# A hybrid attention layer: a differential head's output transposes moved two fillings later, the latent heads' squares summed by ScalarE, latent keys scaled as they leave PSUM

## The chip, the cores and the metric

The kernel runs on one core of one Trainium2 chip. The metric is device time in microseconds of one execution: the median of a few runs, with one more run that was profiled. The traces below are of that profiled run.

## The reference, cut to what matters

One encoder layer over 512 positions of width 2048. Its attention has two groups of 8 heads that share one input projection and one output projection; a SwiGLU feed-forward network follows. All arithmetic is float32.

```python
h = rms_norm(x, g_norm1) * (1 + sc1) + sh1
proj = h @ w_in
...
# differential heads: two softmaxes, one subtracted from the other
a = p[:, 0] - lam * p[:, 1]
a_out = rms_norm(a @ v, g_subln) * (1 - lambda_init)
# latent heads: query and key come from low-rank latents, both are normed
q_m = rms_norm((rms_norm(cq, g_q_a) @ w_q_b), g_q_mla)      # 192 = 128 + 64 rotary
kv = rms_norm(ckv, g_kv_a) @ w_kv_b                         # per head 128 key, 128 value
k_m = rms_norm(concat([k_nope, k_pe]), g_k_mla)             # mean of squares over 192
b_out = latent_attention(q_m, k_m, v_m)
mix = concat([a_out, b_out]) @ w_out
```

The norm of a latent key needs the sum of squares of its 128 own columns plus that of the 64 shared rotary columns, then a power of -0.5, and multiplies the key with it.

## The kernel before, in words

Float32 products are made of three matmuls on parts: a high part `hi` (ScalarE, L89) and a remainder `lo` (VectorE or GpSimd, L97) of each weight chunk, against the same two parts of the activations (`mm3`, L241 to L243).

The order of TensorE's instructions is the order in which the program writes them (`ORDERED` holds TensorE alone). On the other engines the framework's scheduler chooses an order, by program order among the instructions whose inputs and buffers it takes to be ready; so an instruction can stand in a queue ahead of one that the program writes earlier.

The attention part weaves two streams on TensorE. One is the heads' own work, written as a string of steps (`DIFF_STEPS` for a differential head, `MLA_STEPS` for a latent one): `s0` to `s3` are the scores of four blocks of queries, `t` the transposes of the probabilities, `v` the product with the values, `n` the norm of the next head's queries and keys, `o` the next head's operands, `e` the finish of the head before. The other stream is the filling, `F`: projections (`projections`), of which each `F` runs as many matmuls as its share of `DIFF_FILL` or `MLA_FILL` allows. Nine `F` share 26 us in a differential head.

`values` ends a block with a chain: ScalarE squares z with a sum over its columns (L738), GpSimd scales, adds and takes the power (L739 to L741) and multiplies z (L742). `finish` (step `e`) transposes the four z of a head on TensorE (L748, `ps_zT`) and splits the result (L610, L611).

`diff_norm` puts 8 multiplications (L666) and the power of the sums (L260, L261) of a coming head on GpSimd.

`mla_project(pr)` is run by the filling once for each of four pairs of latent heads. It projects queries (`qb`, 4 PSUM banks of tag `acc`), copies them out (`qm`), makes the rotary tails on GpSimd (L765 to L768, L827; eight `dup` buffers, which the pair before gives back when its second head's tails are transposed, L623), squares them (L831), reduces the squares on VectorE (L832), and takes the power on GpSimd (L834 to L836). Then it projects keys and values (`kvb`, the same 4 banks), and for each of four blocks squares the key (L844), reduces (L845), copies the value out (L847) and copies the key out (L813 through `copy`, `kn`). GpSimd adds the rotary squares (L853), takes the power (L260, L261), and multiplies `kn` (L857) and the rotary key (`kpt`, L859). Both PSUM tags, `acc` and `tmp`, have 4 banks. After the second and the fourth pair (pr 1 and 3) the filling goes straight on with a part of the output projection (`out_half`, `ps_o`), which takes 4 banks of `acc` again; after the first and the third it waits for the heads.

Of the kernel before, what the change touches and what calls it, by code (L numbers as in the profile page):

```python
# [12 lines left out]
AF = mybir.ActivationFunctionType  # L13
ALU = mybir.AluOpType
AX = mybir.AxisListType
# [3 lines left out]
P = 128  # L19
# [179 lines left out]
def hybrid_layer(ctx, tc, a, out):  # L199
    nc = tc.nc  # L200
    act, dve, pool, pe, sp = nc.scalar, nc.vector, nc.gpsimd, nc.tensor, nc.sync
# [23 lines left out]
    def bank(tag, name):  # L225
        return psum.tile([P, 512], F32, tag=tag, name=name)
# [31 lines left out]
    def rsqrt(dst, src, scale, eps=EPS):  # L258
        n = src.shape[-1]
        pool.tensor_scalar(out=dst, in0=src, scalar1=scale, scalar2=eps, op0=ALU.mult, op1=ALU.add)  # L260
        pool.tensor_tensor(out=dst, in0=dst, in1=mhalf[:, :n], op=ALU.pow)  # L261
# [145 lines left out]
    i = 0  # L407
    for kind in LOADS:
# [4 lines left out]
        else:  # L413
            t, b = divmod(i, 4)
# [35 lines left out]
    for t in range(NT):  # L450
        for b in range(4):
            sq = st[1].tile([P, 512], F32, tag="sq", bufs=2, name="sq1")
# [10 lines left out]
    def raw_tile(name="raw_in"):  # L463
        return sh[1].tile([P, 384], F32, tag="rin", bufs=16, name=name)

    def project(pss, lhs, width, chunks, k0=0, n=None, first=True, last=True, fine=False):

        n = len(lhs) if n is None else n
        kc = k0
        for key in chunks:  # L470
            wh, wl = W.get(key)
            nk = wh.shape[1]

            def mm(t, i):
                hh, hl = lhs[kc + i]
                mm3(pss[t][:, :width], hh[:, tsl(t)], hl[:, tsl(t)], wh[:, i], wl[:, i],
                    first and kc + i == k0, last and kc + i == k0 + n - 1)

            if kc + nk < k0 + n:
                for i in range(nk):  # L480
                    for t in range(NT):
                        mm(t, i)
                        if fine:
                            yield 3 * width * 0.000424
                    if not fine:
                        yield 12 * width * 0.000424
            else:
                for t in range(NT):
                    for i in range(nk):
                        mm(t, i)  # L490
                    if t % 2 or fine:
                        yield (1 if fine else 2) * 3 * nk * width * 0.000424
            kc += nk
# [96 lines left out]
    def sm(n, tag, bufs=4):  # L590
        return const.tile([P, n], F32, tag=tag, bufs=bufs, name=tag)
# [4 lines left out]
    def dup_tile(name):  # L596
        return sh[1].tile([P, 2, 2, 64], F32, tag="dup", bufs=8, name=name)
# [161 lines left out]
    def rope(dst, src, tb, t, nh):  # L759

        tmp = sh[1].tile([P, 2, 2, 32], F32, tag="rt", bufs=1, name="rt")
        s4 = src.rearrange("p h (s n) -> p h s n", s=2)
        o4 = dst.rearrange("p h (s n) -> p h s n", s=2)
        for i in range(2):
            pool.tensor_tensor(out=tmp[:, :nh, i, :], in0=s4[:, :, 1 - i, :],  # L765
                               in1=tb[1][:, t, i, :].unsqueeze(1).broadcast_to([P, nh, 32]), op=ALU.mult)
        pool.tensor_tensor(out=o4, in0=s4, in1=tb[0][:, t].unsqueeze(1).broadcast_to([P, nh, 2, 32]), op=ALU.mult)
        pool.tensor_tensor(out=o4, in0=o4, in1=tmp[:, :nh], op=ALU.add)  # L768
# [40 lines left out]
    def copy(by_act, dst, src):  # L809
        if by_act:  # L810
            act.copy(out=dst, in_=src)
        else:
            dve.tensor_copy(out=dst, in_=src)  # L813

    def mla_project(pr):
        pss = [bank("acc", "ps_in") for _ in range(NT)]
        yield from project(pss, latT["cq"], 384, [("qb", pr, 0), ("qb", pr, 1)], fine=True)
        qn, qp = [], []
        rs = sm(2 * NT, "rsq", 3)
        for t in range(NT):  # L820
            q = raw_tile("qm")
            copy(Q_ACT[t], q, pss[t][:, :384])
            q = q.rearrange("p (h n) -> p h n", h=2)
            qn.append(q)
            d = dup_tile("qpe")
            rope(d[:, :, 0, :], q[:, :, NOPE:], qtab, t, 2)
            pool.tensor_copy(out=d[:, :, 1, :], in_=d[:, :, 0, :])  # L827
            qp.append(d)
        for t in range(NT):
            sq = wk[1].tile([P, 384], F32, tag="sq", bufs=2, name="sqm").rearrange("p (a b) -> p a b", a=2)  # L830
            act.activation(sq, qn[t], AF.Square)  # L831
            dve.tensor_reduce(out=rs[:, 2 * t:2 * t + 2], in_=sq, axis=AX.X, op=ALU.add)  # L832
        rs2 = rs.rearrange("p (t h) -> p t h", t=NT)
        pool.tensor_scalar(out=rs, in0=rs, scalar1=1.0 / QKH, scalar2=None, op0=ALU.mult)  # L834
        pool.tensor_tensor(out=rs2, in0=rs2, in1=epsq.unsqueeze(2).broadcast_to([P, NT, 2]), op=ALU.add)
        pool.tensor_tensor(out=rs, in0=rs, in1=mhalf[:, :2 * NT], op=ALU.pow)  # L836
        pss = [bank("acc", "ps_in") for _ in range(NT)]
        yield from project(pss, latT["ckv"], 512, [("kvb", pr)], fine=True)
        kn, kp, v = [], [], []
        rk = sm(2 * NT, "rsk", 2)  # L840
        for t in range(NT):
            pv = pss[t].rearrange("p (h s n) -> p h s n", h=2, s=2)
            sq = wk[1].tile([P, 384], F32, tag="sq", bufs=2, name="sqm")[:, :256].rearrange("p (a b) -> p a b", a=2)
            act.activation(sq, pv[:, :, 0, :], AF.Square)  # L844
            dve.tensor_reduce(out=rk[:, 2 * t:2 * t + 2], in_=sq, axis=AX.X, op=ALU.add)  # L845
            vr = sh[1].tile([P, 2, P], F32, tag="v", bufs=8, name="vr")
            act.copy(out=vr, in_=pv[:, :, 1, :])  # L847
            v.append(vr)
            k = raw_tile("kn")[:, :256].rearrange("p (h n) -> p h n", h=2)
            copy(K_ACT[t], k, pv[:, :, 0, :])  # L850
            kn.append(k)
        rk2 = rk.rearrange("p (t h) -> p t h", t=NT)
        pool.tensor_tensor(out=rk2, in0=rk2, in1=sskpe.unsqueeze(2).broadcast_to([P, NT, 2]), op=ALU.add)  # L853
        rsqrt(rk, rk, 1.0 / QKH)
        for t in range(NT):
            r = rk[:, 2 * t:2 * t + 2].unsqueeze(2)
            pool.tensor_tensor(out=kn[t], in0=kn[t], in1=r.broadcast_to([P, 2, P]), op=ALU.mult)  # L857
            d = dup_tile("kpt")
            pool.tensor_tensor(out=d, in0=kpe[:, t:t + 1, :].unsqueeze(1).broadcast_to([P, 2, 2, 64]),  # L859
                               in1=r.unsqueeze(3).broadcast_to([P, 2, 2, 64]), op=ALU.mult)  # L860
            kp.append(d)
        pairs[pr] = (qn, qp, kn, kp, v, rs)
# [123 lines left out]
    def between(us, n):  # L986
        fill.run(us)
        for _ in range(n):
            next(side, None)
# [9 lines left out]
    for h in range(H):  # L999
        cur = diffs[h]  # L1000
        for step in DIFF_STEPS.split():
            kind, i = step[0], int(step[1:] or 0)
            if kind == "F":
                between(DIFF_FILL[h] / DIFF_STEPS.count("F"), DIFF_SIDE[h])
            elif kind == "n":
# [17 lines left out]
    for g in range(H + 1):  # L1023
# [4 lines left out]
        for step in MLA_STEPS.split():  # L1028
            kind, i = step[0], int(step[1:] or 0)
# [35 lines left out]
    def tmp(name):  # L1065
        return fo[1].tile([P, S], F32, tag="tmp", bufs=4, name=name)
# [25 lines left out]
    for b in range(4):  # L1092
        tag = next_tag()
        spare[0] = "tmp" if tag == "acc" else "acc"
        if b == 0:
            assert tag == "acc"
            pss = half[0]
        else:
            pss = [bank(tag, "ps_o") for _ in range(NT)]
        j0 = 0 if b == 1 else 4  # L1100
        for i, _ in enumerate(project(pss, mixT, 512, [("out", b, j) for j in range(j0, 8)], 2 * j0, KC - 2 * j0,
# [6 lines left out]
            if b == 1 and i % 2 and i < 16:  # L1108
                b2, t = 2 + i // 8, i % 8 // 2
# [8 lines left out]
        for t in range(NT):  # L1118
            residual(pss, b, t, gt1, pool if t in OUT_POOL and b < 3 else dve)
            sq = tmp("sq")  # L1120
# [19 lines left out]
    s3 = sx[1].tile([P, 8, 256], F32, name="s3")  # L1140
# [215 lines left out]
    for u in range(N_UNITS):  # L1356
# [4 lines left out]
        else:  # L1361
# [4 lines left out]
                         in_=ao.rearrange("p (f c) s -> p f (c s)", f=2))  # L1366
# [29 lines left out]
    for i, n in enumerate(PARTS):  # L1396
        for b in range(4):
            tag = next_tag()
            spare[0] = "tmp" if tag == "acc" else "acc"
            pss = [bank(tag, "ps_d") for _ in range(NT)]  # L1400
# [11 lines left out]
            for t in range(NT):  # L1412
                s = sums[t][b]
# [22 lines left out]
OUT_POOL = ()  # L1436
OUT_SPLIT = "alt"
Q_ACT = (0, 0, 1, 1)
K_ACT = (0, 0, 0, 0)
GATE_EARLY = True  # L1440
START_FILL = 5.2
DIFF_STEPS = "s0 F e s1 n F t0 F s2 v0 F t1 F s3 v1 F t2 F o0 v2 t3 F o1 v3 F"
DIFF_FILL = (26.0, 26.0, 26.0, 26.0, 26.0, 26.0, 26.0, 26.3)
DIFF_SIDE = (1, 2, 1, 2, 1, 2, 1, 1)
MLA_SIDE = (1, 2)
# [42 lines left out]
```

## Time and profile before

| | |
|---|---|
| median of 3 runs | 2294.44 us (2291.91 to 2295.82) |
| profiled execution, its own time | 2292.43 us |
| its span | 2290.6 us |
| TensorE matmul busy | 2183.1 us (95%) |
| VectorE, ScalarE, GpSimd busy | 71%, 41%, 18% |
| mean granted TensorE clock | 0.988 |

The span is the time between the first and the last instruction of the profiled run; 1.8 us of its time lie around it. TensorE sets the time where its row is full; where its row has gaps, the wait that ends each gap names the engine that was late. The differential heads run from about 240 to 560 us of the span, the latent heads from there to about 775 us. The feed-forward network fills the rest, from about 900 us on.

### The profile page before, as it was taken

The numbers are of one execution on the slowest core, as the hardware profiler recorded it, in microseconds if no ns is written. First come the engines' busy times: TensorE is split into PE (matmuls) and PEld (weight loads), VectorE is DVE, ScalarE is ACT, GpSimd is POOL, SyncE is SP. The second block draws the span as 40 slices with busy tenths as digits, with TensorE's granted clock in tenths as the row PEclk, the third lists the DMA queues.
The fourth block names the chain that finished last, engine by engine and source line by source line (L and its number), as shares of the span: only waits on it lengthen the run. The fifth ranks groups of instructions, "written<-read, shape, count | busy, mean of one in ns | idle before, by whom it ended". The sixth has DMA issues, their size and how long they took to land.

```text
span 2290.6 us, 35353 instructions
## 1 busy us (share of the span) xinstructions
PE 2183.1 (95%) x13878; PEld 1999.4 (87%) x13878; DVE 1625.7 (71%) x2290; ACT 945.3 (41%) x1569; POOL 418.2 (18%) x478
## 2 busy tenths in 40 slices
PE   2899999998989998999999999999999999999999
PEld 2799989997777776889999999999999877888887
DVE  5987788868998477857777777777777577232543
ACT  4423545556555323434444444444444522222221
POOL 0002533436444431000000000000000122222221
PEclk9899999999999998999999999999999999999999
DMA  9975345432433577233333333333333686242542
GB/s 295 330 224 152 92 146 157 136 90 84 161 121 119 173 251 256 85 128 120 130 120 123 110 127 117 119 116 129 120 127 123 218 274 215 101 133 98 165 138 101
DMA packets 270826, 344.99 MB, mean 151 GB/s; under 512 B 15006, under 2 KB 171143, under 8 KB 270531
## 3 DMA queue, kind: packets, MB, share of 16 engines
q1 hardware_dynamic: 267864, 338.18, 45.0%
q10 hardware_dynamic: 2794, 4.55, 0.6%
q8 instruction: 108, 1.77, 0.3%
q14 instruction: 60, 0.48, 0.1%
HBM read 322.71 MB, written 19.96 MB: 150 GB/s over the span
## 4 chain that ended last, share of the span: by engine, by line
PE 60%; DVE 8%; DMA 5%; issue 2%; ACT 1%; SPq 0%; POOL 0%; DVEq 0%; ACTq 0%; POOLq 0%
PE ps_d L243 6%; PE ps_d L242 6%; PE ps_d L241 6%; PE ps_X L1253 5%; PE ps_X L1254 5%; PE ps_X L1255 5%; PE ps_W L1253 3%; PE ps_W L1255 3%; PE ps_W L1254 3%; DVE adaacc L308 3%; DMA araw<-in_w_ada_dram 2%; DMA x<-in_w_ada_dram 2%; PE ps_Z L1253 2%; PE ps_Y L1253 2%; PE ps_Y L1255 2%
## 5 line engine op out<-in xcount | busy, mean ns | idle before, releaser
L89 ACT CAST hi<-raw 128x1024 fp32r<-128x1024 f32 (+2 forms) x228 | 221.3, 971 | 494.5 <-PE ps_d L242 275.1
L97 POOL TENSOR_TENSOR lo<-raw,hi 128x1024 fp32r<-128x1024 f32 (+1 forms) x67 | 161.4, 2410 | 1386.0 <-DMA raw<-in_w_down_dram 879.9
L97 DVE TENSOR_TENSOR lo<-raw,hi 128x1024 fp32r<-128x1024 f32 (+2 forms) x161 | 178.7, 1110 | 168.3 <-ACT hi L89 164.3
L1236 ACT CAST wh<-wr 128x1024 fp32r<-128x1024 f32 x160 | 168.6, 1054 | 242.1 <-PE ps_X L1254 68.3
L1255 PE MATMUL ps_X<-comb,wl 128*128 128x256 f32 x960 | 267.8, 279 | 0.0
L1253 PE MATMUL ps_X<-comb,wh 128*128 128x256 f32 x960 | 267.8, 279 | 0.0
L1254 PE MATMUL ps_X<-comb,wh 128*128 128x256 f32 x960 | 267.8, 279 | 0.0
L243 PE MATMUL ps_d<-lo,ax 128*128 128x512 f32 x640 | 250.4, 391 | 7.6 <-DVE lo L97 7.6
L242 PE MATMUL ps_d<-hi,ax 128*128 128x512 f32 x640 | 249.6, 390 | 0.0
L241 PE MATMUL ps_d<-hi,ax 128*128 128x512 f32 x640 | 249.6, 390 | 0.0
L1219 DVE TENSOR_TENSOR wl<-wr,wh 128x1024 fp32r<-128x1024 f32 x160 | 195.5, 1222 | 74.1 <-ACT wh L1236 73.9
L243 PE MATMUL ps_in<-lo,hh 128*128 128x384 f32 (+2 forms) x704 | 232.7, 331 | 10.9 <-DVE lo L97 10.8
L241 PE MATMUL ps_in<-hi,hh 128*128 128x384 f32 (+2 forms) x704 | 238.0, 338 | 3.5 <-ACT hi L89 2.6
L242 PE MATMUL ps_in<-hi,hl 128*128 128x384 f32 (+2 forms) x704 | 232.0, 330 | 0.8 <-DVE hl L402 0.7
L1236 ACT CAST wh<-wt 128x1024 fp32r<-128x1024 f32 x120 | 126.1, 1051 | 195.2 <-PE ps_X L1254 118.8
L1219 DVE TENSOR_TENSOR wl<-wt,wh 128x1024 fp32r<-128x1024 f32 x120 | 146.7, 1223 | 78.8 <-ACT wh L1236 78.8
L1254 PEld LDWEIGHTS ps_X<-comb,wh 128*128 128x128 f32 x960 | 180.5, 188 | 0.0
L1253 PEld LDWEIGHTS ps_X<-comb,wh 128*128 128x128 f32 x960 | 180.5, 188 | 0.0
L1255 PEld LDWEIGHTS ps_X<-comb,wl 128*128 128x128 f32 x960 | 180.5, 188 | 0.0
L1253 PE MATMUL ps_W<-comb,wh 128*128 128x256 f32 x640 | 178.9, 280 | 0.9 <-DVE cu L1264 0.8
L1255 PE MATMUL ps_W<-comb,wl 128*128 128x256 f32 x640 | 178.5, 279 | 0.0
L1254 PE MATMUL ps_W<-comb,wh 128*128 128x256 f32 x640 | 178.5, 279 | 0.0
(320 smaller groups left out, 5488.7 us busy)
## 6 DMA issues: line engine op xcount, KB each, us to landing
raw<-in_w_down_dram SPq DMA_DIRECT2D x88, 512.0 KB
araw<-in_w_ada_dram SPq DMA_DIRECT2D x80, 512.0 KB
wr<-in_w_gate_dram SPq DMA_DIRECT2D x40, 1024.0 KB
wr<-in_w_up_dram SPq DMA_DIRECT2D x40, 1024.0 KB
ada<-in_w_ada_dram SPq DMA_DIRECT2D x128, 256.0 KB
raw<-in_w_in_dram SPq DMA_DIRECT2D x128, 192.0 KB
raw<-in_w_out_dram SPq DMA_DIRECT2D x32, 512.0 KB
x<-in_w_ada_dram SPq DMA_DIRECT2D x64, 256.0 KB
```

The source lines that it names most:

```text
L89: nc.scalar.copy(out=hi[:, :n], in_=raw[:, :n])
L97: e.tensor_tensor(out=lo[:, :n], in0=raw[:, :n], in1=hi[:, :n].bitcast(F32), op=ALU.subtract)
L241: pe.matmul(o, ah, bh, start=start, stop=False)
L242: pe.matmul(o, al, bh, start=False, stop=False)
L243: pe.matmul(o, ah, bl, start=False, stop=stop)
L308: dve.scalar_tensor_tensor(out=acc[:, :width], in0=raw[:, i, :width], scalar=c_col[:, q:q + 1], in1=acc[:, :width], op0=ALU.mult, op1=ALU.add)
L1219: dve.tensor_tensor(out=out, in0=x, in1=y, op=ALU.subtract)
L1236: act.copy(out=hi, in_=src)
L1253: pe.matmul(ps[bk], wh[:, k], c[:, 0], start=first and k == 0, stop=False, skip_group_check=True)
L1254: pe.matmul(ps[bk], wh[:, k], c[:, 1], start=False, stop=False, skip_group_check=True)
L1255: pe.matmul(ps[bk], wl[:, k], c[:, 0], start=False, stop=k == 7, skip_group_check=True)
```

## The change

`e` stands two `F` later in a head's string. In `mla_project` the squares of each head are one ScalarE instruction that also gives the sum, in place of one instruction for both heads and a reduction on VectorE. The key is no longer copied out of PSUM and multiplied in place on GpSimd: one VectorE multiplication reads it from PSUM, after the power, and writes the scaled key.

```diff
@@ mla_project, queries
-            act.activation(sq, qn[t], AF.Square)
-            dve.tensor_reduce(out=rs[:, 2 * t:2 * t + 2], in_=sq, axis=AX.X, op=ALU.add)
+            for i in range(2):
+                act.activation(sq[:, i], qn[t][:, i], AF.Square, accum_out=rs[:, 2 * t + i:2 * t + i + 1])
@@ mla_project, keys
-            act.activation(sq, pv[:, :, 0, :], AF.Square)
-            dve.tensor_reduce(out=rk[:, 2 * t:2 * t + 2], in_=sq, axis=AX.X, op=ALU.add)
+            for i in range(2):
+                act.activation(sq[:, i], pv[:, i, 0, :], AF.Square, accum_out=rk[:, 2 * t + i:2 * t + i + 1])
             vr = sh[1].tile([P, 2, P], F32, tag="v", bufs=8, name="vr")
             act.copy(out=vr, in_=pv[:, :, 1, :])
             v.append(vr)
-            k = raw_tile("kn")[:, :256].rearrange("p (h n) -> p h n", h=2)
-            copy(K_ACT[t], k, pv[:, :, 0, :])
-            kn.append(k)
@@ after the power
             r = rk[:, 2 * t:2 * t + 2].unsqueeze(2)
-            pool.tensor_tensor(out=kn[t], in0=kn[t], in1=r.broadcast_to([P, 2, P]), op=ALU.mult)
+            k = raw_tile("kn")[:, :256].rearrange("p (h n) -> p h n", h=2)
+            pv = pss[t].rearrange("p (h s n) -> p h s n", h=2, s=2)
+            dve.tensor_tensor(out=k, in0=pv[:, :, 0, :], in1=r.broadcast_to([P, 2, P]), op=ALU.mult)
+            kn.append(k)
@@ constants
-K_ACT = (0, 0, 0, 0)
-DIFF_STEPS = "s0 F e s1 n F t0 F s2 v0 F t1 F s3 v1 F t2 F o0 v2 t3 F o1 v3 F"
+DIFF_STEPS = "s0 F s1 n F t0 F e s2 v0 F t1 F s3 v1 F t2 F o0 v2 t3 F o1 v3 F"
```

## Rows read from the trace of the kernel before

**Rows 1.** The page's first part: busy time, share of the span, instructions.

```profile
PE 2183.1 (95%) x13878; PEld 1999.4 (87%) x13878; DVE 1625.7 (71%) x2290; ACT 945.3 (41%) x1569; POOL 418.2 (18%) x478
```

**Rows 2.** TensorE's waits, 250 to 900 us, then 555 to 565: sum, times, longest.

```profile
PE ps_zT L748 <- POOL z L742: 11.2, 5, 5.7
...
PE ps_zT L748 <- POOL z L742: 1.8, 1, 1.8
```

**Rows 3.** Busy time by stretch: PE, PEld, DVE, ACT, POOL, granted clock, DMA.

```profile
327.00:334.00 7.00, 4.88 (x15) 4.50 (x16) 2.67 (x9) 2.31 (x5) 1.82 (x5) 0.51 0.64 206
...
374.00:382.00 8.00, 8.00 (x39) 7.80 (x39) 5.20 (x12) 3.42 (x7) 0.22 (x1) 0.79 0.78 249
536.00:562.00 26.00, 21.31 (x116) 17.27 (x115) 24.89 (x61) 19.06 (x53) 22.08 (x47) 0.93 0.36 125
...
578.00:600.00 22.00, 19.98 (x92) 15.78 (x91) 21.38 (x40) 10.04 (x22) 20.71 (x32) 0.92 0.57 189
...
640.00:668.00 28.00, 20.86 (x111) 16.18 (x111) 26.34 (x56) 14.26 (x32) 17.59 (x31) 1.00 0.38 122
```

**Rows 4.** The timeline, 320 to 330 us: start, duration, engine, line, idle before.

```profile
320.31 0.33 PE L241 MATMUL ps_in<-hi,hh 128*128 128x384 f32 x1
...
322.93 0.49 PE L748 MATMUL ps_zT<-anti,z 128*128 128x128 f32 x3
...
328.66 0.40 POOL L742 TENSOR_TENSOR z<-z,zs 128x128 f32<-128x128 f32 x1
...
329.12 0.47 PE L748 MATMUL ps_zT<-anti,z 128*128 128x128 f32 x1 [5.70 <-POOL z L742]
```

**Rows 5.** Instructions by tile (squares, keys): duration ns least, median, most; starts.

```profile
L832 DVE TENSOR_REDUCE rsq<-sqm x16: 535/542/553, 536.3 to 686.5; 128x2 f32<-128x384 f32 x16
L844 ACT ACTIVATE sqm<-ps_in x16: 364/384/422, 540.0 to 694.4; 128x256 f32<-128x256 f32 x16
L845 DVE TENSOR_REDUCE rsk<-sqm x16: 390/406/412, 542.5 to 695.5; 128x2 f32<-128x256 f32 x16
...
L813 DVE COPY kn<-ps_in x16: 402/410/416, 543.1 to 696.2; 128x256 f32<-128x256 f32 x16
```

**Rows 6.** Instructions by tile (z): ScalarE squares with a sum over 128 columns.

```profile
L738 ACT ACTIVATE zb<-z x32: 295/311/315, 255.2 to 560.1; 128x128 f32<-128x128 f32 x32
L738 ACT ACTIVATION_READ_ACCUMULATOR zb<-z x32: 185/187/193, 255.4 to 560.3; 128x1 f32 x32
```

**Rows 7.** The timelines of PE and POOL around the second pair, 574 to 602.

```profile
578.87 0.39 PE L243 MATMUL ps_in<-lo,ckvh 128*128 128x512 f32 x1
...
581.49 0.48 PE L241 MATMUL ps_o<-hi,mh 128*128 128x512 f32 x1
...
585.94 2.37 POOL L97 TENSOR_TENSOR lo<-raw,hi 128x1024 fp32r<-128x1024 f32 x1
...
593.06 1.89 POOL L261 TENSOR_TENSOR rsk<-rsk,mhalf 128x8 f32<-128x8 f32 x1
```

**Rows 8.** The timelines of PE and POOL around the fourth pair, 680 to 722.

```profile
691.89 0.40 PE L243 MATMUL ps_in<-lo,ckvh 128*128 128x512 f32 x1
692.13 0.39 PE L241 MATMUL ps_o<-hi,mh 128*128 128x512 f32 x1
...
689.40 0.92 POOL L767 TENSOR_TENSOR qpe<-qm,qtab 128x128 f32<-128x128 f32 x2
...
699.20 2.40 POOL L97 TENSOR_TENSOR lo<-raw,hi 128x1024 fp32r<-128x1024 f32 x1
...
702.55 1.66 POOL L261 TENSOR_TENSOR rsk<-rsk,mhalf 128x8 f32<-128x8 f32 x1
```

**Rows 9.** The timelines of PE and POOL after the first and the third pair.

```profile
562.39 0.42 PE L241 MATMUL ps_in<-hi,cqh 128*128 128x384 f32 x1
...
667.21 0.33 PE L241 MATMUL ps_in<-hi,cqh 128*128 128x384 f32 x1
...
650.08 1.99 POOL L261 TENSOR_TENSOR rsk<-rsk,mhalf 128x8 f32<-128x8 f32 x1
```

## The prediction

> **What bounds the kernel now.** I read the page's first part, then TensorE's waits, then the busy times by stretch, then the timeline at the places the diff names. TensorE's matmuls fill 95% of the span [rows 1], so a cut on another engine counts only where TensorE waits for it. Over the attention part one wait leads TensorE's list: the finish of a differential head (`ps_zT`) waits for GpSimd's last multiplication of z, 11.2 us in five waits, one of them 5.7 us; 1.8 us of it belong to the last head, whose finish lies in the latent heads' string and isn't moved [rows 2]. The timeline of the longest shows the cause: three of four transposes run at 322.9, z is written by 329.06, and TensorE stands until then [rows 4]. A stall also costs afterwards: between 327 and 334 us the granted clock was 0.51, so TensorE, which started again at 329.1, ran at the lower of its two levels for some 4.9 us; after the next long wait the clock was 0.79 over 8 us [rows 3]. In the latent heads' projections VectorE is nearly full (24.9 of 26 us; 26.3 of 28 us) and TensorE has gaps of 4.7 and 7.1 us there [rows 3]: there, unlike elsewhere, VectorE's time matters.
>
> **The change part by part.** Each term is a change of the profiled execution's own 2292.4 us, minus for a gain.
>
> The moved finish. The waits that can go are 11.2 - 1.8 = 9.4 us [rows 2]. One filling lasted 322.93 - 320.31 = 2.6 us [rows 4]. Two of them alone put the transposes, wanted at 322.9, at 328.1; `s1` (four matmuls of 512 columns, 0.39 us each at most [rows 8]) and `t0` put them at up to 330.3. z is there at 329.06. So between nothing and 0.9 us of the longest wait stays, and I take nothing; the shorter waits are well inside the shift. What the move issues is four transposes, one ScalarE split and one VectorE split, all of them there before, and no DMA. The finish takes its `tmp` bank just ahead of `s2`, which takes two, and `v0`, which takes the fourth: with four banks that fits if those of `s1` and `t0` are read within the filling between; I cost it at nothing, at most a VectorE pass or two a head. With the waits goes the low clock: 4.9 us at half speed are 2.4 us, and 8 x 0.21 = 1.7 us [rows 3]. Term: -(9.4 + 2.4 + 1.7) = -13.5, between -9 and -14.
>
> The squares. VectorE loses 16 reductions of 0.542 and 16 of 0.406 us [rows 5], 15.2 us, 3.8 us a pair. ScalarE pays: a square over 128 columns with its sum takes 0.311 us, and the read of the sum 0.187 us, mostly under the next instruction [rows 6]; two of them in place of one of 0.384 us [rows 5] are some 0.24 us more, 32 times with the wider query squares, about 8 us in all. ScalarE is 41% busy [rows 1], so this is hidden except where its sum is awaited, which is counted below. VectorE's 3.8 us come back only where TensorE waits for VectorE. At the first pair (536 to 562) TensorE's gaps are 4.7 us, 1.8 of them the unmoved finish, and its clock 0.93 [rows 2, 3]: I take -2, between 0 and -4.
>
> The keys. VectorE's 16 copies of 0.410 us [rows 5] become 16 multiplications of the same shape from the same bank. No row shows this one; nearest is the copy, and I take the same. GpSimd is rid of 16 multiplications. But the copy was what gave the bank back. Now a bank of `acc` stays taken until the sums of all four blocks are there, GpSimd has taken the power, and VectorE has multiplied. Who wants the banks next? After the first pair a query projection at 562.39, after the third one at 667.21, where the power is done at 652.07 [rows 9]: no stall. After the second pair `ps_o` wants the first bank at 581.49, 2.2 us after the last key matmul's end, 579.26 [rows 7]; after the fourth at 692.13, directly behind the last key matmul, which ends at 692.3 [rows 8]. TensorE is in order: the scores of the next latent head stand behind the stalled `ps_o`, and ScalarE and VectorE behind them.
>
> How long? From below, with every engine free: two squares 0.62, the read 0.19 [rows 6], the two short steps ahead of the power 0.95 (701.60 to 702.55) and the power 1.66 [rows 8], one multiplication 0.41 [rows 5]: 3.8 us after the last key matmul. That is a stall of 1.6 us at the second pair and 4.0 at the fourth. From above, with GpSimd's queue as it was: the power ended at 594.95 and 704.21 [rows 7, 8], so the first bank comes back at 595.4 and 704.6, and the stalls are 13.9 and 12.5 us. What lies between is GpSimd's queue: the query tails (689.40 to 699.20 at the fourth pair) and one weight remainder of 2.4 us [rows 8]. The remainder is written behind the power in the program, but ran ahead of it, at the second pair even amid the tails [rows 7], so the scheduler does put ready work between them, and the sums, freed of VectorE's queue, are ready some microseconds sooner. Nothing in the rows says how far ahead the power moves. I take the middles, 8 us each. At the second pair the stall swallows the 2.0 us of gaps that TensorE has there, and its low clock costs 2.4 in place of 1.8 us (22 x 0.08) [rows 3]: 8 - 2.0 + 0.6 = 6.6. At the fourth 8 + 2.4 = 10.4. Term: +17, between +4 and +30.
>
> At the third pair no bank is wanted, but VectorE is in order too: if the multiplications stand in its queue where the copies stood, it stands until 652.07 [rows 9], and behind it wait the maxima and remainders of the running head's scores, for which TensorE waits. Against that stand the 3.8 us that it is relieved of. I take 0, between -3 and +4. In the two stalls VectorE goes on with the modulation sums of its side work and is ahead afterwards: -1.5, between 0 and -3.
>
> The sum: -13.5 - 2 + 17 + 0 - 1.5 = 0. The profiled execution, 2292.4, stands 2.0 below the median of the runs, inside their spread; I set the forecast between the two, at 2293.
>
> **The rivals.** A difference under about 0.2% (4.6 us) is what a measurement of this kernel can't tell from none, so "same" is 2289.9 to 2299.0.
>
> The power early. The sums are ready before GpSimd is through the tails, and the scheduler puts the power among them. For it: the remainder amid the tails [rows 7]. Against it: the tails come earlier in the program, and at the fourth pair the sums come late. With both stalls at the floor the second vanishes in its 2.0 us of gaps and the fourth costs 4.0 + 1.7: -13.5 - 2 + 5.7 - 1 = -10.8, 2282.
>
> The banks late. This is the one on the other side: the power stays behind tails and remainder, and VectorE is held in order with it. For it: both powers stood there before [rows 7, 8]. Against it: the sums come sooner. At the upper bounds: 13.9 + 0.6 + 12.5 + 2.4 + 4 - 13.5 = +19.9; halfway between that and the forecast's 0, +10, 2302. It decides once the two stalls together pass some 20 us. The Trainium skill (PSUM — Partial Sum Buffer, Summary: rules for kernel authors) says it in three words, "Evacuate promptly", since the buffer is small. By that rule this change, which evacuates after a power on another engine, gives the result of this case, 2302; the trace so far agrees in that a bank is wanted 2.2 us and at once after its last key matmul [rows 7, 8].
>
> The move does nothing. z stays late by as much, if the scheduler puts more of the next head's norm ahead of it: without the 13.5, 2306. Against it: z was ready at 329.06 whatever TensorE did.
>
> **How the numbers follow.** Forecast 0.37, its own range 2287 to 2299; power early 0.32; banks late 0.26; move does nothing 0.05. Faster: a quarter of the forecast and 0.9 of the power early, 0.38. Slower: 0.05 of the forecast, 0.85 of the banks late and the last case, 0.29. Same: the rest, 0.33. The range takes in the early power at its floor and the middle of the late banks: 2282 to 2305.
>
> **What would show it.** No wait of `ps_zT` on GpSimd between 280 and 460 us, and a clock of 1.0 there. Two new waits on TensorE, `ps_o` for VectorE's `kn`, of 5 to 11 us each; under 3 and 5 us the power came early, over 11 us late. VectorE waiting for `rsk` at the third pair would show the hold. The prediction fails if GpSimd's queue is reordered further than the rows let me see, or if the stall at the fourth pair lets later weights arrive early and is paid back after 720 us.

## The result, and the profile after

The change makes the kernel slower: 2315.4 us median against 2295.1 of the kernel before, a ratio of 1.0089 [1.0069, 1.0109], some 20 us. The forecast was 2293 with a range to 2305, so it was wrong, and on the side of the rival "banks late". The profiled execution took 2316.16 us.

The page's first part, in the order of [rows 1], then TensorE's waits between 240 and 920 us (who waited for whom: sum, times, longest):

```profile
span 2314.4 us, 35376 instructions
PE 2191.4 (95%) x13878; PEld 2008.1 (87%) x13878; DVE 1605.9 (69%) x2258; ACT 951.6 (41%) x1665; POOL 397.4 (17%) x462
...
PE ps_o L241 <- DVE kn L856: 19.4, 2, 9.9
PE ps_s L241 <- DVE aTl L608: 4.4, 1, 4.4
PE ps_z L732 <- DVE aTl L608: 3.7, 4, 2.3
PE ps_s L699 <- DVE cf L708: 3.6, 1, 3.6
...
PE ps_zT L748 <- POOL z L742: 1.8, 1, 1.8
```

VectorE is 20 us less busy, GpSimd 21, and the time shows neither. Of the five waits of `ps_zT` [rows 2] only the 1.8 us of the last head is left, as predicted. In their place stand the two predicted waits of `ps_o` for VectorE's `kn`, and three groups of waits for VectorE that the sum of the prediction did not hold: 3.7 us of `ps_z`, most of it at the tenth head; 3.6 us of `ps_s` at the first pair, where VectorE stands 2.30 us on the power and no stall was booked; and 4.4 us at the third pair, behind the hold that the prediction named and put at 0. The stretches, with columns as in [rows 3]:

```profile
327.00:334.00 7.00, 7.00 (x45) 6.80 (x44) 5.37 (x16) 5.02 (x14) 1.07 (x3) 1.00 0.54 145
374.00:382.00 8.00, 7.96 (x47) 7.34 (x46) 6.68 (x15) 4.12 (x10) 1.91 (x4) 1.00 0.76 240
380.00:390.00 10.00, 7.66 (x39) 7.27 (x37) 9.53 (x20) 3.32 (x9) 1.86 (x4) 0.83 0.90 284
540.00:550.00 10.00, 6.38 (x28) 5.35 (x27) 7.54 (x23) 6.35 (x21) 6.62 (x13) 0.66 0.01 2
580.00:592.00 12.00, 5.54 (x17) 4.44 (x18) 6.12 (x13) 0.87 (x2) 8.33 (x17) 0.57 0.48 162
650.00:660.00 10.00, 5.57 (x26) 4.47 (x26) 6.34 (x15) 2.38 (x7) 7.30 (x12) 0.66 0.27 79
700.00:716.00 16.00, 7.70 (x26) 6.18 (x27) 11.22 (x22) 3.10 (x10) 10.09 (x14) 0.68 0.40 135
```

The clock is back at 1.00 where the finishes stalled (0.51 and 0.79 in [rows 3]), and it is low in the other five, one beside each new stall (a mean between its two levels): in the trace of before it was 1.00 in four of them and 0.86 at the second pair.

The timelines of the four engines around the second and the fourth pair and, between them, VectorE at the third (start, duration, and in brackets the idle time before):

```profile
574.03 0.39 PE L243 MATMUL ps_in<-lo,ckvh 128*128 128x512 f32 x1
...
575.48 1.12 ACT L89 CAST hi<-raw 128x1024 fp32r<-128x1024 f32 x1
...
577.64 0.36 ACT L845 ACTIVATE sqm<-ps_in 128x128 f32<-128x128 f32 x1
577.80 0.30 ACT L845 ACTIVATION_READ_ACCUMULATOR sqm<-ps_in 128x1 f32 x1
...
577.16 0.96 DVE L308 SCALAR_TENSOR_TENSOR ada<-ada,c_col 128x512 f32<-128x512 f32 x1 [2.56 <-DMA ada<-in_w_ada_dram]
...
578.81 2.33 POOL L97 TENSOR_TENSOR lo<-raw,hi 128x1024 fp32r<-128x1024 f32 x1
...
584.19 1.67 POOL L261 TENSOR_TENSOR rsk<-rsk,mhalf 128x8 f32<-128x8 f32 x1
...
585.89 1.09 DVE L856 TENSOR_TENSOR kn<-ps_in,rsk 128x256 f32<-128x256 f32 x3 [4.73 <-POOL rsk L261]
...
586.46 0.76 PE L241 MATMUL ps_o<-hi,mh 128*128 128x512 f32 x1 [9.57 <-DVE kn L856]
...
653.54 0.42 DVE L856 TENSOR_TENSOR kn<-ps_in,rsk 128x256 f32<-128x256 f32 x1 [5.00 <-POOL rsk L261]
...
698.02 0.40 PE L243 MATMUL ps_in<-lo,ckvh 128*128 128x512 f32 x1
...
701.49 0.27 ACT L845 ACTIVATE sqm<-ps_in 128x128 f32<-128x128 f32 x1
...
703.01 2.51 POOL L97 TENSOR_TENSOR lo<-raw,hi 128x1024 fp32r<-128x1024 f32 x1
...
706.04 1.65 POOL L261 TENSOR_TENSOR rsk<-rsk,mhalf 128x8 f32<-128x8 f32 x1
707.73 1.42 DVE L856 TENSOR_TENSOR kn<-ps_in,rsk 128x256 f32<-128x256 f32 x4 [4.41 <-POOL rsk L261]
...
708.30 0.77 PE L241 MATMUL ps_o<-hi,mh 128*128 128x512 f32 x1 [9.88 <-DVE kn L856]
```

From the end of the last key matmul, 574.42, to `ps_o` at 586.46 are 12.0 us; with all engines free the prediction's floor was 3.8. ScalarE reached the fourth block's squares late (sums complete at 578.10, not some 0.8 us behind the matmul), since a weight rounding and two casts stood in between. GpSimd was then in the weight remainder and the tails, and did the power only at 584.19. That is 8.9 us earlier than before the change [rows 7], 4.8 of them since TensorE is ahead, and still far too late.

**Where the time goes.** One table carries the study: the start of the same TensorE step in each profile minus its start in the profile of before, at ten steps (scores and out-projection matmuls; the first row is their start in before) and at the end of the span. The columns are the places between which time is won or lost.

```
           first   lead   10th/11th  ahead of  after  after   ahead of  after  after   end of   span
           step    most   head       1st pair  1st    2nd     3rd       3rd    4th     out-pr.
before    239.80  383.61   450.90     544.32  580.67  603.41  640.61   689.79  711.23  895.21  2290.6
after      -0.8   -12.0     -5.8       -6.3    -4.8    +2.6    +2.6     +6.2   +17.0   +17.2   +23.8
e1 move    -0.6   -12.4     -5.1       -5.6    -4.0    -5.2    -5.3     -4.3    -4.8    -3.4    +1.5
e2 squares -0.4    -1.3     -1.2       -1.0    -1.9    -4.1    +0.8     +5.5    +5.0    +4.3    +4.7
e3 keys    +1.5    +0.4     +0.4       +0.7    +4.2    +9.0    +9.4    +12.1   +23.7   +25.0   +29.6
e4 no keys -0.1   -11.8     -4.1       -4.3    -3.6    -4.9    -3.6     -0.4    -1.1    -0.9    +0.4
e5 no pow. +0.3   -11.6     -4.6       -4.9    -6.0    -1.3    -1.0     -0.9    +7.6    +7.3    +7.2
e6 copy    +0.0   -12.0     -4.1       -4.4    -1.9    +3.5    +3.7     +5.9   +11.2   +11.3   +10.8
e8 no loads-1.3    -1.6     -1.6       -1.3    -1.5    -2.6    +3.0     +5.1    +4.3    +4.5    +3.9
e9 e4, none+0.6   -11.1     -8.9       -8.2    -6.9    -7.9    -6.9     -7.1    +1.7    +2.9    +8.8
e10 1st,3rd+0.9   -10.3     -3.4       -3.7    -2.3    -2.0    +2.9     +6.6    +7.0    +7.5   +11.9
e11 ahead  +0.3    -9.6     -5.7       -5.8    -2.8    -4.1    -4.2     -1.0    -1.2    -0.9   +35.1
e12 e4, ah.+0.6    -8.4     -5.0       -5.4    -3.3    -4.3    -1.9     +5.2   +13.3   +13.3   +49.6
```

The last two columns differ by 6.6 us in the changed kernel: that is the feed-forward part, whose code is the same. In the profiles of e1 to e10 this difference runs from -2.1 (e7) to +5.9 (e9) in no order of the edits (e4 has +1.3). It goes with the execution that was profiled: the five that took longer than their kernel's median (the whole change, e1, e3, e9 and e10) have +4.4 to +6.6, the six that lay 2.4 to 9.5 us under it have -2.1 to +1.3. e11 and e12 are a case of their own (below). So profiles are compared up to the end of the out-projection, and times by the medians.

### The profile page after: what moved, and what is told of

Its sections match the earlier page's. It is cut to its first block, busy times and chain, and to the rows that moved or that the text cites. A ratio compares the mean times of both kernels' runs of the same rounds, so it can differ in the third digit from the quotient of the medians.

```text
span 2314.4 us, 35376 instructions
## 1 busy us (share of the span) xinstructions
PE 2191.4 (95%) x13878; PEld 2008.1 (87%) x13878; DVE 1605.9 (69%) x2258; ACT 951.6 (41%) x1665; POOL 397.4 (17%) x462
## 4 chain that ended last, share of the span: by engine, by line
PE 58%; DMA 6%; DVE 6%; issue 2%; POOL 2%; ACT 1%; SPq 0%; DVEq 0%; ACTq 0%; POOLq 0%
PE ps_d L243 5%; PE ps_d L242 5%; PE ps_d L241 5%; PE ps_X L1253 5%; PE ps_X L1255 5%; PE ps_X L1254 5%; PE ps_W L1253 3%; PE ps_W L1255 3%; PE ps_W L1254 3%; DVE adaacc L308 2%; DMA araw<-in_w_ada_dram 2%; DMA x<-in_w_ada_dram 2%; PE ps_Z L1253 2%; PE ps_Z L1255 2%; PE ps_Z L1254 2%
```

## The experiments

The theory after the result: the late banks and the held VectorE cost all of the loss and more, and the other two parts gain about what was forecast. Against it stand rivals by which the finish gives nothing in the end (A) or hurts (B), by which ScalarE's doubled squares make everything late (C), or by which the loss is partly behind the attention part (D); E to G come with their experiments.

**One part at a time.** e1, e2 and e3 are the kernel before with one part each; e4 is the change without its key part.

```
e1:  DIFF_STEPS = "s0 F s1 n F t0 F e s2 v0 F ..."          (nothing else)
e2:  act.activation(sq[:, i], ..., AF.Square, accum_out=...)  (twice a block, for queries and keys)
e3:  dve.tensor_tensor(out=k, in0=pv[:, :, 0, :], in1=r..., op=ALU.mult)   (VectorE's reductions stay)
e4:  the change, with copy(K_ACT[t], k, pv[:, :, 0, :]) and GpSimd's kn *= rsk as before
```

> Only the later finish. Theory (the key multiplications cost all of the loss and more): the waits of ps_zT between 280 and 460 us are gone, TensorE is 9 to 12 us ahead at 371 us as in the whole change, no ps_o wait on kn; about 5 us may be given back at the tenth head, so 5 to 12 us faster than before (2283 to 2290). Rival A (the move does nothing in the end, because VectorE is late with the transposed weights after it): within 3 us of before. Rival B (the move itself hurts through the tmp banks): over 3 us slower.

> Only the squares summed by ScalarE. Theory: 15 us less on VectorE, which TensorE hardly waits for: between 0 and 4 us faster (2291 to 2295), no ps_o wait over 2 us. Rival C (ScalarE, with twice as many squares out of PSUM, is the late engine and holds the banks): over 4 us slower, with new waits of TensorE on ScalarE or on kn.

> Only the keys scaled on the way out of PSUM; the squares are still summed by VectorE's reductions. Theory: ps_o waits of 9 to 14 us on kn at the second and the fourth pair and VectorE standing 2 to 5 us on rsk at the first and the third: 20 to 30 us slower than before (2315 to 2325), with the reductions making the sums later than in the whole change. Rival C (the squares on ScalarE make the sums late): ps_o waits under 6 us in sum and within 10 us of before.

> The whole change with the keys as before: copied out of PSUM by VectorE, multiplied by GpSimd. Theory: no ps_o wait on kn over 2 us, VectorE does not stand on rsk; the lead of the finish is kept: 5 to 13 us faster than before (2282 to 2290), over 25 us faster than the whole change. Rival A: within 3 us of before. Rival D (some 6 us of the loss lie behind the attention part, whatever the keys do): the last feed-forward matmul is again 6 us later against the end of attention than before.

Measured: e1 0.9978 [0.9968, 0.9987], 5 us faster. e2 1.0015 [1.0004, 1.0025], 3 us slower. e3 1.0091 [1.0076, 1.0105], 21 us slower. e4 1.0000 [0.9989, 1.0011]. By the ratios, on a median of 2298, the parts add up to -5.1 + 3.4 + 20.9 = +19, against the +20 of the whole. The keys carry the loss; the theory stands there: e3 is as slow as expected with the squares still on VectorE, its two stalls of `ps_o` are 7.4 and 11.2 us, 18.6 in sum against the 19.4 of the whole, and so rival C fell for the keys. The theory was wrong on the squares, which were expected to gain and cost 3 us, just short of rival C's 4, though the new waits of TensorE in e2 are for VectorE and not for ScalarE. And the finish keeps 5.1 us of the 12.4 that it wins (the column "lead most" against "10th/11th head"): e1 is at the lower edge of what was expected, and e4 missed. It came out as rival A has it, equal to before, and 20 us, not over 25, under the whole. Rival D fell: e4 loses 1.3 us behind the attention part.

Where e1 gives its lead back, SyncE's DMA queue, VectorE and TensorE in its timeline:

```profile
366.24 1.30 SPq L301 DMA_DIRECT2D ada<-in_w_ada_dram  x3
...
379.08 0.75 DVE L308 SCALAR_TENSOR_TENSOR ada<-ada,c_col 128x512 f32<-128x512 f32 x1 [0.99 <-DMA ada<-in_w_ada_dram]
...
380.56 0.75 DVE L308 SCALAR_TENSOR_TENSOR ada<-ada,c_col 128x512 f32<-128x512 f32 x1 [0.65 <-DMA ada<-in_w_ada_dram]
...
383.70 0.68 DVE L608 TENSOR_TENSOR aTl<-ps_aT,aTh 128x512 fp32r<-128x512 f32 x1
...
384.43 0.66 PE L732 MATMUL ps_z<-v,aTl 128*128 128x128 f32 x4 [2.77 <-DVE aTl L608]
```

The first load of that block and the same remainder in the timeline of before:

```profile
374.53 0.36 SPq L301 DMA_DIRECT2D ada<-in_w_ada_dram  x1
...
390.58 0.69 DVE L608 TENSOR_TENSOR aTl<-ps_aT,aTh 128x512 fp32r<-128x512 f32 x1
```

TensorE is 12 us early, and VectorE is not. The modulation block's loads come 8.3 us earlier (366.24 against 374.53); VectorE stands for two of them, 1.64 us, and goes through modulation sums (L308) and other remainders first; the remainder of the transposed probabilities, for which TensorE waits 2.77 us, comes 6.9 us earlier (383.70 against 390.58). e2 shows a like case with VectorE early instead of TensorE; the timelines of GpSimd, SyncE's DMA queue, VectorE and TensorE:

```profile
603.26 2.41 POOL L97 TENSOR_TENSOR lo<-raw,hi 128x1024 fp32r<-128x1024 f32 x1 [4.84 <-ACT hi L89]
...
605.70 0.38 SPq L73 DMA_DIRECT2D raw<-in_w_kv_b_dram  x1
606.13 2.94 SPq L301 DMA_DIRECT2D ada<-in_w_ada_dram  x6
...
611.22 1.29 DVE L308 SCALAR_TENSOR_TENSOR ada<-ada,c_col 128x512 f32<-128x512 f32 x1 [3.21 <-DMA ada<-in_w_ada_dram]
...
613.74 0.73 DVE L611 SCALAR_TENSOR_TENSOR kTl<-ps_kT,small,kTh 128x512 fp32r<-128x512 f32 x1
...
614.53 0.56 PE L243 MATMUL ps_s<-kTl,qTh 128*128 128x512 f32 x1 [3.37 <-DVE kTl L611]
```

The relieved VectorE runs into a modulation block whose load stands in SyncE's queue behind a weight load, which waits for its staging buffer: GpSimd reads that buffer until 605.67. The remainder that TensorE needs stands behind all that. Up to 603 us the squares had gained 4.1 us, about what the prediction allowed at most, though 2.2 of it came at the second pair and not at the first, where it was expected; this place and the third pair, where VectorE stands another 2.59 us on such a load, take 9.6.

**Without the loads.** Do those loads take the gains? In the kernel before (e8) and in e4 (e9) each modulation sum beside the attention loads one block and sums it 16 times.

```
 for j in range(KC // nq):
-    raw = raws(); sp.dma_start(out=raw, in_=w_ada[...])
+    if j == 0 or raws is not slot_of:
+        raw = raws(); sp.dma_start(out=raw, in_=w_ada[...])
```

> The kernel before, but each modulation sum that runs beside the attention reads one loaded block of its weights over and over: the loads of the other blocks are left out, VectorE's instructions are all there. Theory (VectorE seldom stands for these loads in the kernel before, 5.5 us in nine waits): 0 to 6 us faster than before.

> The later finish and the squares on ScalarE, keys as before, with the modulation loads left out in the same way. Theory (VectorE, once ahead, stands in order before a modulation block that is not loaded, and so gives back what the two edits gained): without these loads the lead stays, 8 to 15 us faster than the kernel before with the same loads left out, where the two edits with the loads give 0. Rival E (the order of VectorE's instructions at the tenth head and the third pair gives it back, the loads do not matter): within 4 us of the kernel before with the loads left out.

Measured: e8 1.0026 [1.0012, 1.0041], e9 1.0011 [0.9995, 1.0027]; e9 is 3 us faster than e8, not 8 to 15, which is in the range of rival E, and e8 is slower than before: both expectations missed. The traces say why. From the first step to 706 us e9 gains 14.4 us on e8 (e4 gained 1.0 on before): 11.5 up to 382 us, of which 2.1 are given back by 402 (e4: 5.8 by 410), and 4.8 more between 603 and 633. Those 4.8 are e8's loss and not e9's gain: e9 loses 0.5 us there against before, e8 5.3, at the place where e2 lost. Then one wait of 7.53 us, with the low clock behind it, takes 9.9 of it; GpSimd and TensorE in e9:

```profile
700.09 2.78 POOL L97 TENSOR_TENSOR lo<-raw,hi 128x1024 fp32r<-128x1024 f32 x1
...
702.93 0.79 PE L243 MATMUL ps_o<-lo,mh 128*128 128x512 f32 x1 [7.53 <-POOL lo L97]
```

TensorE, ahead, now needs an out-projection weight whose remainder stands in GpSimd's queue behind tails and key multiplications. VectorE and TensorE in e8, where it loses:

```profile
607.04 2.32 DVE L309 SCALAR_TENSOR_TENSOR ada<-ada,c_col 128x512 f32<-128x512 f32 x3
609.27 0.75 DVE L612 SCALAR_TENSOR_TENSOR qTl<-ps_qT,small,qTh 128x512 fp32r<-128x512 f32 x1
...
610.08 0.50 PE L241 MATMUL ps_s<-kTh,qTh 128*128 128x512 f32 x1 [1.57 <-DVE qTl L612]
```

VectorE stands for no load there, and TensorE still waits 1.57 us, then 2.13 us at 616.62, for remainders that stand behind modulation sums: VectorE's order alone costs, as rival E has it. At the tenth head the loads do take a part of the lead (2.1 us given back without them, 5.8 with them, and before the fourth pair e9 is 7.1 us ahead of before where e4 is 0.4). How the rest is shared between loads and order these runs don't show; that the absence of the loads makes the kernel faster is not shown either, since another in-order queue takes the lead next.

**Loading ahead.** The same cause tried with all the work done: each modulation block is loaded two blocks ahead of the one summed, in e1 (e11) and in e4 (e12). The lines below show the constant too, and the line of the feed-forward part that reads it, which the edit leaves as it is.

```
-AHEAD = 2
+AHEAD = 3
...
+    while len(loaded) < min(j + (AHEAD if raws is slot_of else 1), KC // nq):
+        raw = raws()...; sp.dma_start(out=raw, in_=w_ada[...]); loaded.append(raw)
+    raw = loaded[j]
...
             prepare(q + AHEAD)
```

> Only the later finish, and each modulation block beside the attention is loaded two blocks ahead of the one that is summed, so that its load stands further ahead in SyncE's queue of weight loads. Theory (the lead of the later finish is given back where VectorE stands in order for a modulation block): VectorE's waits on these loads, 9.3 us between 236 and 730 us, fall below 4, the lead at 410 us stays near 10 us instead of 6.5, and the kernel is 2 to 5 us faster than the later finish alone, 8 to 12 us faster than before. Rival E (the order of VectorE's instructions gives it back): the lead at 410 us is 6 to 7 us again, and the time within 2 us of the later finish alone, 5 us faster than before.

> The later finish and the squares on ScalarE, keys as before, with the same loads two blocks ahead. Theory: the loss of 5 us at the third pair, where VectorE stood for a modulation block, goes: 6 to 12 us faster than before, where without the loads ahead it was 0. Rival E: within 3 us of before.

Measured: e11 1.0128 [1.0114, 1.0142], e12 1.0200 [1.0186, 1.0215]: 29 and 46 us slower. At the tenth head e11 gives back 2.4 us, not 6.0 as e1 does. But between 330 and 348 it has already lost 2.2 us more than e1, and at the end of the out-projection it stands at -0.9 (e1: -3.4): the wait is moved, not removed. VectorE's waits for these loads fell to 6.2 us, not under 4, and the lead at 410 us is 7.2 us, not near 10. In e12 the third pair and a wait for GpSimd's weight remainder take 17 us. Then both lose 36 us in the feed-forward part. TensorE's waits there in e11, where e1 has 1.4 us in 2 waits of this kind:

```profile
PE ps_W L1257 <- DVE cu L1268: 20.4, 39, 2.3
```

The edit did more than load ahead. `AHEAD` is a name that the kernel has already: it sets how many products ahead the feed-forward network prepares its weights, in three buffers each. With 3 in place of 2 that preparation moved too, and in e11 VectorE runs four preparing passes ahead of the `cu` that TensorE waits for (1203 to 1208 us). The rest of the feed-forward code is that of e1, so this is the likely cause of the 36 us; no run parts the two changes. The two times therefore say nothing about loading ahead. By the profiles up to the end of the out-projection, where the table can be read, it did not help: e11 is 2.5 us behind e1, e12 14 behind e4.

**The key part taken apart.** e6 copies each key block out of PSUM and lets VectorE multiply it in place behind the power. e10 has the new keys at the first and third pair only. e5 takes GpSimd out of the chain (and leaves the power out). e7 writes the query tails behind the power.

```
e6:  dve.tensor_copy(out=k, in_=pv[:, :, 0, :]); ...; dve.tensor_tensor(out=kn[t], in0=kn[t], in1=r..., op=ALU.mult)
e10: if pr in (1, 3): copy out, pool.tensor_tensor(kn[t] *= r)   else: as in the change
e5:  dve.tensor_tensor(rk2 += sskpe); dve.tensor_scalar(rk = rk * 1/QKH + EPS)     (no power)
e7:  the loop of rope() and pool.tensor_copy for qpe moved behind rsqrt(rk, ...)
```

> The whole change, but each key block is first copied out of PSUM by VectorE and then multiplied in place by VectorE after the power. The banks come back early; VectorE still stands in order for the power. Theory (two costs, bank stalls and VectorE's hold): no ps_o wait on kn, VectorE's waits on rsk at three or four pairs stay at 2 to 5 us each, so between the two: 2300 to 2308, some 10 us faster than the whole change and some 5 to 10 slower than the version with the keys as before. Rival F (only the banks matter): as the version with the keys as before, 2297 within 3. Rival G (only the hold matters): as the whole change, 2315 to 2320.

> The whole change with the query tails of GpSimd written behind the power of the keys, so that GpSimd has nothing of the tails in its queue when the key sums come. Theory (GpSimd's queue holds the power): the ps_o waits on kn fall from 9.6 and 9.9 us to 2 to 5 each, some 10 us faster than the whole change (2303 to 2310); the tails come later, and the second pair's query transposes may wait for them. Rival C (the squares on ScalarE set the power's time, not GpSimd's queue): the waits stay over 7 us each.

> The whole change, with the two short steps on the key sums done by VectorE, and the power left out (the keys are multiplied by the mean square itself). GpSimd is out of the chain from the sums to the key multiplications. Theory (GpSimd's queue of tails and a weight remainder holds the sums): the ps_o waits on kn fall from 9.6 and 9.9 us to under 5 each, at the second pair to about what the late squares of the fourth block leave, 2 to 4; VectorE no longer stands on rsk; 12 to 20 us faster than the whole change (2295 to 2303). Rival C (the squares on ScalarE set the time): the waits stay over 7 us and the total within 5 us of the whole change.

> The whole change with the new keys at the first and third pair only; at the second and fourth, where ps_o wants the banks, they are copied out and multiplied by GpSimd as before. Theory (19 us of bank stalls at these two, 4 to 8 us of VectorE's hold at the other two): no ps_o wait on kn, VectorE stands 2 to 5 us on rsk at the first and third pair and TensorE is held there; 12 to 18 us faster than the whole change, 2298 to 2306, slower than the version with all keys as before (2297) by 2 to 8. Rival F (the banks are all of it): 2297 within 2.

Measured: e6 1.0055 [1.0036, 1.0074]; e10 1.0020 [1.0004, 1.0035]; e5 1.0031 [1.0021, 1.0041]; e7 1.0084 [1.0058, 1.0110].

e6 and e10 came out as the theory said, between e4 and the whole: banks and VectorE's order both cost. In e6 no `ps_o` waits over 0.5 us for `kn`, yet VectorE stands 10.5 us on the power at three pairs, 4.4 of them at the second, with the running head's probabilities (`pm`) behind it, and TensorE waits 4.5 for those. Giving the bank back early saves about 8 of the 20 us, and leaves e6 13 us above e4, more than the 5 to 10 expected. Keeping the old keys at the two pairs where `ps_o` follows (e10) saves 16. What is left against e4, 5 us, can't be put down to VectorE's hold at the other two pairs: by the table most of it (3.6 us) is lost between 603 and 641 us, ahead of the third pair's power, where VectorE stands 2.56 us on a modulation load and TensorE 3.37 us behind it, as in e2; against e4 the first pair costs 0.7 and the third 0.5.

e7 decides nothing: the scheduler put most of the tails ahead of the power again, and the waits of `ps_o` stayed (19.8 us in two).

e5 corrected the theory. The time came out as expected, 13 us faster than the whole change, but the waits did not fall below 5. TensorE's waits, then VectorE and GpSimd at the fourth pair:

```profile
PE ps_o L241 <- DVE kn L856: 15.0, 2, 8.4
...
694.97 0.34 DVE L850 TENSOR_TENSOR rsk<-rsk,sskpe 128x8 f32<-128x8 f32 x1
...
696.33 2.30 DVE L851 TENSOR_SCALAR rsk<-rsk 128x8 f32<-128x8 f32 x1
...
699.21 1.40 DVE L856 TENSOR_TENSOR kn<-ps_in,rsk 128x256 f32<-128x256 f32 x4
...
696.09 2.51 POOL L97 TENSOR_TENSOR lo<-raw,hi 128x1024 fp32r<-128x1024 f32 x1
```

With GpSimd's tails, remainder and power out of the chain, 15.0 of the 19.4 us stay. The rest of each stall is ScalarE's queue (in both kernels the fourth block's sums are complete 3.4 to 3.7 us behind their matmul) and VectorE's own, where remainders, modulation sums and a load stand ahead of the four multiplications. GpSimd isn't wholly out of it either: the short step L851, 0.17 to 0.28 us at the other pairs, took 2.30 beside GpSimd's weight remainder (see the last section), some 2 of the 8.4 us. So it is not "GpSimd's queue" alone that holds the bank, but a chain over three in-order engines, each of which arrives late. Rival C holds only in that ScalarE is one of them: e3, with its squares as before, has stalls of the same size. What e5 saves lies by the table at all four pairs, 2.6, 2.7, 3.5 and 2.3 us; at the first and the third VectorE no longer stands on the power (2.30 and 5.00 us in the whole change).

e1, the later finish alone, is the version that beats both kernels: 0.9978 of before, and 25 us under the whole change by the ratios.

## Why the prediction was wrong

**The step that failed** is the term of the moved finish, "-(9.4 + 2.4 + 1.7) = -13.5, between -9 and -14". The waits went and the clock came back as written: TensorE was 12 us ahead at 384 us, which is 1.7 short of the term. The step took what TensorE wins at one place as won at the end. e1 gives 5.1 us [3.0, 7.4], outside its bounds. The prediction looked for what makes the finish late and did not ask who would be late next once TensorE ran 12 us early: VectorE, whose remainders stand in order behind modulation sums and the loads of these, and which came only 7 us earlier at the tenth head. The waits for those loads stood in the trace of before too, but small: 5.4 us in nine between 236 and 730 us, where e1 has 8.4 in 13 and e4 12.9 in 12.

**The squares** failed in sign: "-2, between 0 and -4", and with them "-1.5" for a VectorE that is ahead. Alone they cost 3.4 us [0.9, 5.8]. VectorE lost the 15 us of work and gained 4 us for TensorE up to 603 us; then, early, it stood 3.21 us on a load with TensorE's remainder behind it. Being ahead was booked as a gain and there became a loss. At the third pair several things meet (e2 loses 4.7 us there, the whole change 3.6, e1 1.0, e5 nothing); which share is the held VectorE's and which the loads' can't be read from these runs.

**The keys** were right in mechanism and near in size: +17 predicted in the range 4 to 30, 21 measured alone. The stalls were 9.6 and 9.9 us where 8 each were taken; by the table the second pair cost 7.4 (predicted 6.6) and the fourth 10.9 (10.4). The middle between floor and ceiling was a fair choice, though for another reason than given: not GpSimd's queue alone, but ScalarE's and VectorE's as well; that the middle came so near is in part luck. VectorE waited for `rsk` at the third pair, as the last part of the prediction asked for, 5.00 us; it waited 2.30 at the first pair too, where the term held nothing, and e3 loses 3.5 us there by the table.

**The sum**: of the 22 us between forecast and result, 8 are the finish, 7 the squares with the "ahead" term, 4 the keys; the rest lies within the uncertainty of the medians. A forecast of no change was the difference of large terms, of which one lasted. The rival "banks late" had the sign and the place, but its 2302 to 2312 also counted on the whole -13.5. The Trainium skill's rule cited there (PSUM — Partial Sum Buffer, Summary: rules for kernel authors, "Evacuate promptly") agrees with the runs: undoing that one part (e4) is worth 20 us.

## What to carry to other kernels

Time won by one engine is kept only if every in-order queue that feeds it can come early as well: list what the others stand on (here modulation sums and their loads ahead of VectorE's remainders, and a weight remainder behind GpSimd's tails) before a gain is booked to the end. Work taken off an engine that isn't the bound can cost, when the engine then reaches a waiting instruction sooner and holds up what stands behind it. A PSUM bank should not wait for a result that passes through three engines if a copy of 0.41 us [rows 5] frees it; but the copy alone (e6) won back 8 of 20 us, since the engine that multiplies afterwards stood in order for the same power. An edit that takes a new name for a constant should look whether the kernel has that name.

## What the runs showed of the hardware

A VectorE step on eight columns (128x8, L851 in e5) took 2.30 us at the fourth pair and ended at 698.63, with GpSimd's weight remainder, which ran from 696.09 to 698.60; at the other pairs, with no remainder beside it, the same step took 0.17 to 0.28. The trace of before shows it on another step: L602, 0.28 us as a rule, took 2.39 at 629.15 and 2.32 at 699.43, and each time ended some 0.15 us behind a GpSimd remainder. The Trainium skill (GPSIMD Engine Reference, Specifications) says that GpSimd shares its SBUF interfaces with VectorE; the trace agrees in that the two ends in e5 lie within 0.03 us, though these runs don't show the mechanism. So a small VectorE step on a chain can cost as much as the power that it replaces (1.66 us in [rows 8]), if a GpSimd pass over a large tile lies beside it.
